# The first 100 microseconds of a one-core encoder layer: queue order of its loads, per-head constants, and the normed input in two VectorE operations

## Chip, cores, metric

The kernel runs on one core of a Trainium2 chip. The metric is the device time of one execution in microseconds, lower is better. A core has five instruction queues that matter here: TensorE (PE, matrix products), VectorE (DVE), ScalarE (ACT), GpSimd (POOL) and SyncE (SP, which in this kernel issues the DMA transfers). Each runs its own instructions in order and waits for the others through semaphores.

## What is computed

One layer of an encoder over 1024 tokens of 1024 channels. A conditioning vector c gives six modulation vectors, x is normed and modulated, and one wide projection feeds a sparse attention branch and a state-space (SSD) branch; then come a merge and a feed-forward part. What the change touches is the first lines:

```python
mod = (jax.nn.silu(c) @ ada_w + ada_b)[:, None, :]
shift_m, scale_m, gate_m, shift_f, scale_f, gate_f = jnp.split(mod, 6, axis=-1)
h = rmsnorm(x, pre_norm_mix) * (1.0 + scale_m) + shift_m
proj = h @ w_in
...
dt = jax.nn.softplus((dt_raw + dt_bias).astype(jnp.float32))
A = -jnp.exp(a_log.astype(jnp.float32))
...
y = (y_diag + y_off).reshape(Bsz, L, SSD_HEADS, SSD_HEADDIM) + d_skip[:, None] * xh
```

`dt_bias`, `a_log` and `d_skip` are the per-head constants, 32 numbers each.

## The kernel before

The kernel holds activations transposed: channels on the 128 partitions, tokens along the free axis. x and h are 8 tiles k = 0 to 7 of 128 channels, each in two halves b of 512 tokens. Products run in a split form: a float32 operand is kept as a high part (rounded to `F32R`, made by ScalarE) and a low part (operand minus high part), and three matmuls, high x high, high x low, low x high, give one product.

The beginning works tile by tile. For each k:

- `k_load(k)` issues three transfers on SP: two of 512 KB with the modulation weights that give scale and shift of tile k (`ada`), and one of 192 KB with tile k of the projection's first 384 columns (`p1raw`). The `ada` tiles come from an arena R of 8 slots, two per k, so the loads of k+4 wait until the matmuls of k have read theirs.
- `k_ada(k)` (through `ada_mm`) multiplies silu(c) with these weights on PE: 16 records in the profile; ScalarE copies the result (`adaacc`).
- `k_mod(k)` (through `ada_end`) sums it up by four tiny matmuls and writes `mod` (shift) and `amul` (gain times 1+scale) on DVE; it then splits `p1raw` into `p1h` (ACT) and `p1l` (POOL).
- `k_h(k, b)` makes the normed input: x times the spread 1/rms `rx[b]` (DVE), the high part `h..h` = x*amul+mod (ACT), the same sum in float32 (DVE), and the low part `h..l` (DVE for b = 0, POOL for b = 1).
- `k_mm(k, b)` accumulates nine matmuls into three PSUM banks (`pp`).

`rx[b]` needs the sums of squares of all eight tiles of that half (`x_squares`, `rstd`, `rspread`), with a power on POOL (`r`). Half 0 is ready first; k = 0 and 1 are done for it alone, then for half 1, and from k = 2 on both halves run in one loop.

Behind the beginning come the other columns of the projection. Their weights are streamed (class `Stream`, called `W`: load `wraw`, high part `whi` on ACT, low part `wlo` on POOL, with 4, 3 and 3 buffers; `uraw`, `uh`, `ul` are the like for a smaller array). `ada_slow` makes the later modulation vectors from `adaw` loads with products on POOL.

What sets the order: a scheduler orders each engine's instructions from dependencies and its own timeline simulation. In the block of the beginning, `in_order(*ORDERED)` chains PE, ACT and DVE to the order in which the code is written. `barrier` names one instruction per engine, and everything wrapped in `behind(...)` (the W stream, the small weights, the `adaw` loads) is put after it on that engine. The barrier stands on SP at the last `k_load`, on ACT and POOL at `k_h(5, 1)`. POOL and SP are not chained in the beginning: what is not named in a barrier may be moved.

`const_loads()` loads the causal mask and the per-head constants in five transfers, straight behind the second half of x. The two of `d_skip` read every second of 32 numbers for each of 64 partitions.

Of the kernel before, what the change touches and what calls it, by code (L numbers as in the profile page):

```python
# [10 lines left out]
F32 = mybir.dt.float32  # L11
# [57 lines left out]
def build(tc, a, dbg=None, stop=99, slots=None):  # L69
# [23 lines left out]
    def f(x):  # L93
        return x.bitcast(F32)
# [91 lines left out]
    ident = con.tile([P, P], F32, name="ident")  # L186
    mask384 = con.tile([P, 384], F32, name="mask384")
    tri = mask384[:, 0:128]
    dtb = con.tile([P, 32], F32, name="dtb")
    alb = con.tile([P, 32], F32, name="alb")  # L190
    dsk = con.tile([P, 16], F32, name="dsk")
    ones = con.tile([P, P], F32, name="ones")
    V.memset(ones, 1.0)
    nhalf = con.tile([P, 8], F32, name="nhalf")
# [117 lines left out]
    def ada_slow(j):  # L312

        acc = EV("adas", (P, 2, P))
        for h in range(2):
            t = wp.tile([P, 4, P], F32, name="adaw", tag="adaw", bufs=2)
            behind(SP.dma_start(t, a["ada_w"][j - 16][:, 4 * h:4 * h + 4]))
            G.tensor_tensor(t, t, cs[:, 4 * h:4 * h + 4, None].to_broadcast([P, 4, P]), op=OP.mult)  # L318
            V.tensor_reduce(acc[:, h], t.rearrange("p k m -> p m k"), axis=AX.X, op=OP.add)
        G.tensor_tensor(acc[:, 0], acc[:, 0], acc[:, 1], op=OP.add)  # L320
        return j, acc[:, 0]

    AHEAD = 2
    X0 = [[None, None] for _ in range(KT)]
    rx, Hs, first = [None, None], [([None, None], [None, None]) for _ in range(KT)], {}

# [12 lines left out]
            sums[k % 2] = sq  # L339

    def k_load(k):
        ts = [R(f"ada{k}", (P, 4, 256)) for _ in range(2)]
        for i in range(2):
            SP.dma_start(ts[i], a["ada_p"][k][i])
        raw = EV("p1raw", (P, 3, P))
        i = SP.dma_start(raw, a["w_p1"][k])
        first[k] = ts, raw
        return i

    def k_ada(k):  # L350
        first[k] = ada_mm(k, first[k][0]), first[k][1]
# [1 line left out]
    def k_mod(k):  # L353
        acc, raw = first[k]
        ada_end(k, acc)
        first[k] = split(Q, raw, "p1", (P, 3, P), lo_eng=G)

    def k_h(k, b):
        x = X0[k][b]
        V.tensor_tensor(x, x, rx[b], op=OP.mult)  # L360
        hi, lo = H_(f"h{k}h", dt=F32R), H_(f"h{k}l", dt=F32R)
        i1 = S.activation(hi, x, AF.Identity, bias=mod[:, k:k + 1], scale=amul[:, k:k + 1])
        V.tensor_scalar(x, x, amul[:, k:k + 1], mod[:, k:k + 1], op0=OP.mult, op1=OP.add)
        i2 = (G if b else V).tensor_tensor(lo, x, f(hi), op=OP.subtract)
        if k == 5:
            barrier.update((i.ins.engine, i.ins.name) for i in (i1, i2))
        Hs[k][0][b], Hs[k][1][b] = hi, lo
        dump("h", x, (k, slice(None), half(b)))

    def k_mm(k, b):  # L370
        for i, (wi, xi) in enumerate(((0, 0), (1, 0), (0, 1))):
# [1 line left out]
                T.matmul(pp1[t][b], first[k][wi][:, t, :], Hs[k][xi][b], start=k == 0 and i == 0, stop=k == KT - 1 and i == 2)  # L373

    def const_loads():
        SP.dma_start(mask384, a["mask384"])
        SP.dma_start(dtb, a["dt_bias"][None, :].to_broadcast([P, 32]))
        SP.dma_start(alb, a["a_log"][None, :].to_broadcast([P, 32]))
        for e in range(2):
            SP.dma_start(dsk[64 * e:64 * e + 64],  # L380
                         a["d_skip"].rearrange("(j e) -> e j", e=2)[e:e + 1, :].to_broadcast([64, 16]))

    x_load(0)
    SP.dma_start(ident, a["ident"])
    for k in range(AHEAD):
        k_load(k)
    x_load(1)
    const_loads()
    with in_order(*ORDERED):
        sums = [None, None], [None, None]  # L390
        x_squares(0, range(8), sums[0])
        r0 = rstd(sums[0], D)
        k_ada(0)
# [12 lines left out]
        k_mm(1, 0)
        r1 = rstd(sums[1], D)
        k_load(2)
        k_ada(2)
        pr1 = rspread(r1)  # L410
        rx[1] = Q("rx")
        S.activation(rx[1], pr1, AF.Copy)
        k_mod(2)
        k_h(0, 1)
        k_h(1, 1)
        k_mm(0, 1)
        k_mm(1, 1)
        for k in range(AHEAD, KT):
            k_h(k, 0)
            k_h(k, 1)  # L420
            if k < KT - 1:
                i = k_load(k + 1).ins
                barrier[i.engine] = i.name
                k_ada(k + 1)
            k_mm(k, 0)
            if k < KT - 1:
                k_mod(k + 1)
            k_mm(k, 1)
        nA = con.tile([P, 32], F32, name="nA")
        S.activation(nA, alb, AF.Exp)  # L430
# [1008 lines left out]
def arrays_of(inp):  # L1439
# [52 lines left out]
```

## Time and profile before

| | |
|---|---|
| median of 3 runs | 2513.75 us (2513.33 to 2513.93) |
| profiled execution, first to last instruction (span) | 2510.1 us; no other time of this execution is listed |
| PE busy | 2394.6 us, 95% of the span |
| DVE, ACT, POOL busy | 1512.3, 1213.8, 1003.9 us |
| the first of 40 slices of the span (63 us) | PE 4 tenths busy, all others 8 or 9 |

How to read the profile: the page gives the busy time of each engine, and the same over 40 slices of the span, a digit for tenths. The table of waits names who waited for whom, with the total in us, how often, and the longest. The timeline gives start and length in us, engine, source line, operation, output and inputs by the program's names, and in brackets the idle time of the engine before it with what ended it. A windows row gives, for one stretch, its length, the busy time of PE, weight loads, DVE, ACT and POOL (with instruction counts), the granted PE clock (1.00 is full), the share in which the 16 DMA engines were busy, and GB/s. A busy PE is not PE at its peak: at half clock it is as busy.

### The profile page before, as it was taken

To read this page: it belongs to the slowest core of one execution; us is meant where nothing else is said; L and a number is where in the kernel's file an instruction comes from. 1 tells how busy PE (TensorE), PEld (TensorE's weight loads), DVE (VectorE), ACT (ScalarE), POOL (GpSimd) and SP (SyncE) were. 2 spreads that over 40 slices of the span, in tenths; PEclk is the share of its full clock that TensorE was granted. 3 is DMA by queue.
4 is the path that set the end of the run, shared out by engine and by line. 5 is a ranking of instruction groups with operands and counts; after the bars stand their busy time and mean duration, and the time that the engine had idled before them with its cause. 6 is when DMAs were issued, how large, how long until landed. Compare 5 with 4: busy or idle time off the path is not lost. (4 is left out here: it accounts for less than half of the span.)

```text
span 2510.1 us, 34872 instructions
## 1 busy us (share of the span) xinstructions
PE 2394.6 (95%) x11946; PEld 1940.7 (77%) x11946; DVE 1512.3 (60%) x3056; ACT 1213.8 (48%) x2300; POOL 1003.9 (40%) x833
## 2 busy tenths in 40 slices
PE   4999999999989999999999999999999999999997
PEld 2788888888767787777776777878777888888886
DVE  3356777499766666866457677354376666442336
ACT  3355666467555665555656565444354222343111
POOL 1332112222443434522335435666576555432233
PEclk7999999999999999999999999999999999999998
DMA  6123212422322223312668885554464444243132
GB/s 243 40 84 130 74 63 76 151 93 97 118 97 91 91 95 123 106 39 69 190 219 283 278 263 179 190 190 135 137 215 157 162 147 143 89 163 131 47 101 89
DMA packets 213026, 338.11 MB, mean 135 GB/s; under 512 B 22976, under 2 KB 87152, under 8 KB 212848
## 3 DMA queue, kind: packets, MB, share of 16 engines
q1 hardware_dynamic: 212128, 335.30, 40.3%
q8 instruction: 94, 1.54, 0.2%
q14 instruction: 84, 0.69, 0.1%
q10 hardware_dynamic: 720, 0.58, 0.1%
HBM read 252.68 MB, written 86.27 MB: 135 GB/s over the span
## 5 line engine op out<-in xcount | busy, mean ns | idle before, releaser
L153 POOL TENSOR_TENSOR wlo<-wraw,whi 128x512 fp32r<-128x512 f32 (+1 forms) x282 | 379.4, 1347 | 761.8 <-ACT whi L152 702.5
L152 ACT ACTIVATE whi<-wraw 128x512 fp32r<-128x512 f32 (+1 forms) x282 | 175.4, 624 | 359.0 <-PE pfo L227 114.2
L1255 PE MATMUL p<-xh,wr 128*128 128x512 f32 x880 | 276.4, 392 | 5.7 <-DVE g L1305 4.2
L1249 POOL TENSOR_TENSOR wr<-a,wr 128x512 fp32r<-128x512 f32 x110 | 153.8, 1410 | 118.6 <-ACT wr L1248 76.6
L1255 PEld LDWEIGHTS p<-xh,wr 128*128 128x128 f32 x880 | 166.5, 189 | 41.7 <-DVE g L1305 4.6
L1255 PE MATMUL p<-xl,wr 128*128 128x512 f32 x440 | 172.2, 391 | 0.0
L779 ACT ACTIVATE lg<-lg,mx 128x256 f32<-128x256 f32 (+7 forms) x128 | 98.4, 770 | 92.3 <-DVE mx L776 90.0
L1248 ACT ACTIVATE wr<-a 128x512 fp32r<-128x512 f32 x110 | 67.9, 628 | 135.5 <-PE p L1255 110.4
L227 PE MATMUL pfo<-ah,wlo 128*128 128x512 f32 x304 | 118.1, 389 | 0.0
L227 PE MATMUL pfo<-al,whi 128*128 128x512 f32 x304 | 117.9, 389 | 0.0
L227 PE MATMUL pfo<-ah,whi 128*128 128x512 f32 x304 | 117.8, 389 | 0.0
L1255 PE MATMUL p<-h2h,wr 128*128 128x512 f32 x352 | 112.0, 394 | 0.0
L1370 DVE TENSOR_TENSOR facc<-facc,pfo 128x512 f32<-128x512 f32 x64 | 43.9, 687 | 112.0 <-PE pfo L227 112.0
L639 ACT ACTIVATE junk<-acc,cand__2203 128x1024 bf16<-128x1024 f32 (+2 forms) x96 | 86.2, 898 | 45.6 <-DVE cand__2203 L682 28.6
L800 PE MATMUL pt<-ident,lg 128*128 128x128 f32 x576 | 89.7, 279 | 15.2 <-ACT lg L779 14.0
L227 PE MATMUL pos<-yh,wlo 128*128 128x512 f32 x256 | 101.0, 395 | 2.7 <-POOL wlo L153 2.7
L227 PE MATMUL pos<-yh,whi 128*128 128x512 f32 x256 | 100.9, 395 | 1.7 <-ACT yh L1121 1.2
L590 DVE SCALAR_TENSOR_TENSOR acc<-rel,widx,acc 128x384 f32<-128x384 f32 (+2 forms) x90 | 87.0, 986 | 24.9 <-ACT rel L585 24.8
L585 ACT ACTIVATE rel<-prel 128x512 f32<-128x512 f32 (+3 forms) x160 | 77.2, 524 | 48.5 <-PE prel L584 45.0
L227 PE MATMUL pos<-yw,whi 128*128 128x512 f32 x256 | 100.3, 393 | 0.0
L318 POOL TENSOR_TENSOR adaw<-adaw,cs 128x512 f32<-128x512 f32 x64 | 68.6, 1075 | 70.2 <-DMA adaw<-ada_w 68.3
L1255 PEld LDWEIGHTS p<-xl,wr 128*128 128x128 f32 x440 | 83.2, 189 | 17.3
(568 smaller groups left out, 7023.7 us busy)
## 6 DMA issues: line engine op xcount, KB each, us to landing
wraw<-w_in SPq DMA_DIRECT2D x130, 256.0 KB, 2.7
a<-w_ffn_in SPq DMA_DIRECT2D x120, 256.0 KB, 3.0
adaw<-ada_w SPq DMA_DIRECT2D x64, 256.0 KB, 2.8
al<-d_ac SPq DMA_DIRECT2D x32, 512.0 KB, 5.7
wraw<-w_o_ssd SPq DMA_DIRECT2D x64, 256.0 KB, 3.0
al<-d_a SPq DMA_DIRECT2D x44, 256.0 KB, 4.9
d_a<-g SPq DMA_DIRECT2D x38, 256.0 KB, 2.0
ada<-ada_p SPq DMA_DIRECT2D x16, 512.0 KB, 7.4
```

Of the source, the lines that this page charges most:

```text
L152: behind(S.activation(hi[:, :kt], raw[:, :kt], AF.Copy))
L153: behind(G.tensor_tensor(lo[:, :kt], raw[:, :kt], f(hi[:, :kt]), op=OP.subtract))
L227: T.matmul(o, wt[:, k0 + i, :], xs[k][xi][b][:, sl], start=pi == 0 and i == 0 and wt is hi and xi == 0, stop=pi == len(pcs) - 1 and i == l ...
L318: G.tensor_tensor(t, t, cs[:, 4 * h:4 * h + 4, None].to_broadcast([P, 4, P]), op=OP.mult)
L585: S.activation(rel[:, 512 * b:512 * b + w_], pr[:, 0:w_], AF.Relu)
L590: V.scalar_tensor_tensor(acc[i][:, 0:n], rel[:, 0:n], ws, acc[i][:, 0:n], op0=OP.mult, op1=OP.add)
L639: S.activation(jk, y, AF.Sign, scale=-1.0, bias=a_, accum_out=o)
L779: S.activation(lg[:, 0:n], lg[:, 0:n], AF.Exp, scale=-1.0, bias=m, accum_out=mx[:, 3:4])
L800: T.transpose(ptv[:, hh, t, :], PR[hh, t][:, j * P:(j + 1) * P], ident)
L1248: S.activation(w[:, 0], src, AF.Copy)
L1249: G.tensor_tensor(w[:, 1], src, f(w[:, 0]), op=OP.subtract)
L1255: T.matmul(p, w[:, wi, i], X[x][i][xi], start=start and i == 0 and k == 0, stop=i == 3 and k == 2, skip_group_check=True)
```

## The change

- The three per-head constants become one array `heads` of 128 x 80 numbers, laid out on the host, so that one transfer of plain rows brings them; `dtb`, `alb`, `dsk` are slices of its tile. It and the mask are issued last, behind the weights of k = 7.
- SP is chained to the written order too, and four groups k are loaded ahead of the loop instead of two; in a group `p1raw` goes first.
- The normed input takes two DVE operations: x*amul*rx, and (x+mod)-high for the low part. ACT's high part adds `mod` alone. POOL makes no low parts of h any more.
- The barriers: on SP the last DMA of the last `k_load`; on ACT `k_h(6, 1)` instead of `k_h(5, 1)`; on POOL the last `p1l`, of k = 7. The POOL products of `ada_slow` now stand behind the barrier as well.

```diff
-            G.tensor_tensor(t, t, cs[:, 4 * h:4 * h + 4, None].to_broadcast([P, 4, P]), op=OP.mult)
+            behind(G.tensor_tensor(t, t, cs[:, 4 * h:4 * h + 4, None].to_broadcast([P, 4, P]), op=OP.mult))
...
-    AHEAD = 2
+    AHEAD = 4
...
     def k_load(k):
+        raw = EV("p1raw", (P, 3, P))
+        SP.dma_start(raw, a["w_p1"][k])
         ts = [R(f"ada{k}", (P, 4, 256)) for _ in range(2)]
         for i in range(2):
-            SP.dma_start(ts[i], a["ada_p"][k][i])
-        raw = EV("p1raw", (P, 3, P))
-        i = SP.dma_start(raw, a["w_p1"][k])
+            last = SP.dma_start(ts[i], a["ada_p"][k][i])
         first[k] = ts, raw
-        return i
+        return last
...
     def k_mod(k):
         acc, raw = first[k]
         ada_end(k, acc)
-        first[k] = split(Q, raw, "p1", (P, 3, P), lo_eng=G)
+        hi, lo = Q("p1h", (P, 3, P), F32R), Q("p1l", (P, 3, P), F32R)
+        S.activation(hi, raw, AF.Copy)
+        i = G.tensor_tensor(lo, raw, f(hi), op=OP.subtract)
+        barrier[i.ins.engine] = i.ins.name
+        first[k] = hi, lo
 
     def k_h(k, b):
         x = X0[k][b]
-        V.tensor_tensor(x, x, rx[b], op=OP.mult)
         hi, lo = H_(f"h{k}h", dt=F32R), H_(f"h{k}l", dt=F32R)
-        i1 = S.activation(hi, x, AF.Identity, bias=mod[:, k:k + 1], scale=amul[:, k:k + 1])
-        V.tensor_scalar(x, x, amul[:, k:k + 1], mod[:, k:k + 1], op0=OP.mult, op1=OP.add)
-        i2 = (G if b else V).tensor_tensor(lo, x, f(hi), op=OP.subtract)
-        if k == 5:
-            barrier.update((i.ins.engine, i.ins.name) for i in (i1, i2))
+        V.scalar_tensor_tensor(x, x, amul[:, k:k + 1], rx[b], op0=OP.mult, op1=OP.mult)
+        i = S.activation(hi, x, AF.Identity, bias=mod[:, k:k + 1])
+        V.scalar_tensor_tensor(lo, x, mod[:, k:k + 1], f(hi), op0=OP.add, op1=OP.subtract)
+        if k == 6:
+            barrier[i.ins.engine] = i.ins.name
...
     def const_loads():
+        SP.dma_start(heads, a["heads"])
         SP.dma_start(mask384, a["mask384"])
-        SP.dma_start(dtb, a["dt_bias"][None, :].to_broadcast([P, 32]))
-        SP.dma_start(alb, a["a_log"][None, :].to_broadcast([P, 32]))
-        for e in range(2):
-            SP.dma_start(dsk[64 * e:64 * e + 64],
-                         a["d_skip"].rearrange("(j e) -> e j", e=2)[e:e + 1, :].to_broadcast([64, 16]))
...
-    for k in range(AHEAD):
+    for k in range(2):
         k_load(k)
     x_load(1)
-    const_loads()
-    with in_order(*ORDERED):
+    for k in range(2, AHEAD):
+        k_load(k)
+    with in_order(*ORDERED, mybir.EngineType.SP):
...
-        k_load(2)
         k_ada(2)
...
-        for k in range(AHEAD, KT):
+        for k in range(2, KT):
             k_h(k, 0)
             k_h(k, 1)
+            if AHEAD <= k + 2 < KT:
+                i = k_load(k + 2).ins
+                barrier[i.engine] = i.name
+            if k + 2 == KT:
+                const_loads()
             if k < KT - 1:
-                i = k_load(k + 1).ins
-                barrier[i.engine] = i.name
                 k_ada(k + 1)
```

How this moves instructions shows at three places. First SP's queue behind the last transfer of x. Before, from there on (`dsk` are the two transfers of `d_skip`, the `ada` tiles 327 and 328 are of k = 2, 402 and 403 of k = 3, `wraw` and `uraw` are the later stage's weights):

```order
L376 DMA mask_90<-mask 128x384
L377 DMA dtb<-dt_bias 128x32
L378 DMA alb<-a_log 128x32
L380 DMA dsk<-d_skip 64x16x1 x2
L344 DMA ada_327<-ada_p 128x1024
L344 DMA ada_328<-ada_p 128x1024
L346 DMA p1raw<-w_p 128x384
L344 DMA ada_402<-ada_p 128x1024
L344 DMA ada_403<-ada_p 128x1024
L346 DMA p1raw<-w_p 128x384 x5
L151 DMA wraw<-w_in 128x512 x2
L167 DMA uraw<-w_qidx 128x512
```

Now, from the same place (`ada` 169 and 170 are of k = 2, 175 and 176 of k = 3, 397 and 398 of k = 4):

```order
L342 DMA p1raw<-w_p 128x384
L345 DMA ada_169<-ada_p 128x1024
L345 DMA ada_170<-ada_p 128x1024
L342 DMA p1raw<-w_p 128x384
L345 DMA ada_175<-ada_p 128x1024
L345 DMA ada_176<-ada_p 128x1024
L342 DMA p1raw<-w_p 128x384
L345 DMA ada_397<-ada_p 128x1024
L345 DMA ada_398<-ada_p 128x1024
```

and nine transfers further on, with the weights of k = 7 (`ada` 559 and 560):

```order
L345 DMA ada_559<-ada_p 128x1024
L345 DMA ada_560<-ada_p 128x1024
L377 DMA heads<-heads 128x80
L378 DMA mask_90<-mask 128x384
L151 DMA wraw<-w_in 128x512 x2
L167 DMA uraw<-w_qidx 128x512
L151 DMA wraw<-w_in 128x512 x2
L316 DMA adaw<-ada_w 128x512 x2
```

The constants went from ahead of k = 2 to behind k = 7, and the later stage's weights, which stood ahead of the `ada` tiles of k = 4 and more, now follow the constants.

Second, POOL from the `r` of half 1 on (`adaw` is `ada_slow`'s product, `h0l` to `h2l` are low parts of half 1). Before:

```order
L266 TENSOR_TENSOR r<-v,nhalf 128x4
L318 TENSOR_TENSOR adaw<-adaw,cs 128x512 x2
L248 TENSOR_TENSOR p1l<-p1raw,p1h 128x384
L364 TENSOR_TENSOR h0l<-x_153,h0h 128x512
L364 TENSOR_TENSOR h1l<-x_155,h1h 128x512
L364 TENSOR_TENSOR h2l<-x_157,h2h 128x512
```

Now:

```order
L265 TENSOR_TENSOR r<-v,nhalf 128x4
L357 TENSOR_TENSOR p1l<-p1raw,p1h 128x384 x6
L317 TENSOR_TENSOR adaw<-adaw,cs 128x512 x2
L153 TENSOR_TENSOR wlo<-wraw,whi 128x512 x2
L169 TENSOR_TENSOR ul<-uraw,uh 128x512
L153 TENSOR_TENSOR wlo<-wraw,whi 128x512 x4
```

The low parts of h are gone from POOL, and `adaw` and the W splits stand behind all `p1l`.

Third, ACT around tiles 5 to 7. Before:

```order
L302 ACTIVATE adaacc<-adap 128x256
L247 ACTIVATE p1h<-p1raw 128x384
L152 ACTIVATE whi<-wraw 128x512 x2
L168 ACTIVATE uh<-uraw 128x512
L152 ACTIVATE whi<-wraw 128x512
L362 ACTIVATE h6h<-x_136,mod,amul 128x512
L362 ACTIVATE h6h<-x_165,mod,amul 128x512
```

Now:

```order
L365 ACTIVATE h6h<-x_134,mod 128x512
L365 ACTIVATE h6h<-x_163,mod 128x512
L301 ACTIVATE adaacc<-adap 128x256
L356 ACTIVATE p1h<-p1raw 128x384
L152 ACTIVATE whi<-wraw 128x512 x2
L168 ACTIVATE uh<-uraw 128x512
L152 ACTIVATE whi<-wraw 128x512
L365 ACTIVATE h7h<-x_136,mod 128x512
```

The first splits of W moved from ahead of tile 6 to ahead of tile 7. On PE, four W matmuls now stand between the products of tile 6 and those of tile 7; behind the next stage's first tiles the order of every engine is the one before.

More of the change, by code (lines that the diff above doesn't have):

```diff
@@ L188, in build @@
     tri = mask384[:, 0:128]
-    dtb = con.tile([P, 32], F32, name="dtb")
-    alb = con.tile([P, 32], F32, name="alb")
-    dsk = con.tile([P, 16], F32, name="dsk")
+    heads = con.tile([P, 80], F32, name="heads")
+    dtb, alb, dsk = heads[:, 0:32], heads[:, 32:64], heads[:, 64:80]
     ones = con.tile([P, P], F32, name="ones")
@@ L355, in k_mod @@
         ada_end(k, acc)
-        first[k] = split(Q, raw, "p1", (P, 3, P), lo_eng=G)
+        hi, lo = Q("p1h", (P, 3, P), F32R), Q("p1l", (P, 3, P), F32R)
[3 more added lines that the diff above has]
+        first[k] = hi, lo
     def k_h(k, b):
         x = X0[k][b]
-        V.tensor_tensor(x, x, rx[b], op=OP.mult)
         hi, lo = H_(f"h{k}h", dt=F32R), H_(f"h{k}l", dt=F32R)
-        i1 = S.activation(hi, x, AF.Identity, bias=mod[:, k:k + 1], scale=amul[:, k:k + 1])
-        V.tensor_scalar(x, x, amul[:, k:k + 1], mod[:, k:k + 1], op0=OP.mult, op1=OP.add)
-        i2 = (G if b else V).tensor_tensor(lo, x, f(hi), op=OP.subtract)
-        if k == 5:
-            barrier.update((i.ins.engine, i.ins.name) for i in (i1, i2))
+        V.scalar_tensor_tensor(x, x, amul[:, k:k + 1], rx[b], op0=OP.mult, op1=OP.mult)
[3 more added lines that the diff above has]
+            barrier[i.ins.engine] = i.ins.name
         Hs[k][0][b], Hs[k][1][b] = hi, lo
-        dump("h", x, (k, slice(None), half(b)))
     def k_mm(k, b):
@@ L1466, in arrays_of @@
     out["vec"] = np.ascontiguousarray(np.concatenate([per_part(parts[n]) for n in COLS], 1))
-    for n in ("rel_bias", "dt_bias", "a_log", "d_skip"):
-        out[n] = np.ascontiguousarray(g[n])
+    out["rel_bias"] = np.ascontiguousarray(g["rel_bias"])
+    rows = np.concatenate([g["dt_bias"], g["a_log"]])[None, :]
+    skip = g["d_skip"].reshape(16, 2).T
+    out["heads"] = np.concatenate([np.repeat(rows, P, 0), np.repeat(skip, 64, 0)], 1)
     out["ident"] = np.eye(P, dtype=f32)
```

## Prediction

> **What bounds the kernel now.** First the page: how busy is TensorE (PE), and where not.
>
> ```profile
> span 2510.1 us, 34872 instructions
> PE 2394.6 (95%) x11946; PEld 1940.7 (77%) x11946; DVE 1512.3 (60%) x3056; ACT 1213.8 (48%) x2300; POOL 1003.9 (40%) x833
> ...
> PE   4999999999989999999999999999999999999997
> ```
>
> PE sets the end nearly everywhere, and the one slice far under nine tenths is the first, which the change edits. So I read PE's waits there (total, times, longest), and those from 105 to 600 us, to see whether a gain at the start is kept.
>
> ```profile
> PE adap L299 <- DMA ada<-ada_p: 12.9, 1, 12.9
> ...
> PE pp L373 <- POOL h0l L364: 9.4, 1, 9.4
> ...
> PE adap L308 <- ACT adaacc L302: 1.8, 1, 1.8
> PE pp L373 <- DVE h6l L364: 1.0, 1, 1.0
> ```
> ```profile
> PE pw L227 <- DVE cv L906: 0.9, 1, 0.9
> ```
>
> One wait for modulation weights, one for POOL, two small ones at tile 6; behind them 495 us with 0.9 us of waiting. From there on the order of every engine is what it was, so what is won earlier moves the rest forward whole.
>
> Why did the weights of k=2 come late? DMA-queue issues; landing times of `dsk`; packets of 22 to 38 us; two stretches whose last two numbers are DMA share and GB/s:
>
> ```profile
> 19.56 1.43 SPq L380 DMA_DIRECT2D dsk<-d_skip  x2
> 21.03 4.34 SPq L344 DMA_DIRECT2D ada<-ada_p  x2
> ```
> ```profile
> DMA to landing us min/median/max: 13.2/18.1/23.0
> ```
> ```profile
> DMA packets 1801, 0.03 MB, mean 2 GB/s; under 512 B 1795, under 2 KB 1800, under 8 KB 1801
> ```
> ```profile
> 4.00:22.00 18.00, 10.65 (x60) 7.64 (x61) 6.39 (x12) 8.66 (x16) 2.02 (x2) 1.00 1.00 359
> 22.00:38.00 16.00, 7.88 (x36) 6.54 (x34) 6.05 (x12) 4.35 (x9) 2.17 (x2) 0.74 0.05 2
> ```
>
> After 359 GB/s the transfers almost stop for 16 us: 1801 packets, nearly all under 512 B and 0.03 MB together, at a share of 0.05, about one engine of 16. They fit `dsk`, two issues of 64x16 single numbers, the last landing near 43 us; `ada` of k=2 was issued behind them at 21.03 and PE got it at 44.71. The timeline of PE, from three windows (start, length, line, operation, output<-inputs, count of matmuls; in brackets the idle time before and who ended it):
>
> ```profile
> 29.96 1.84 PE L261 MATMUL p<-ones,sq 128*128 128x1 f32 x16
> 44.71 2.30 PE L299 MATMUL adap<-ada,cs 128*32 128x256 f32 x16 [12.91 <-DMA ada<-ada_p]
> ...
> 50.60 1.65 PE L373 MATMUL pp<-h0h,p1h 128*128 128x512 f32 x3 [1.90 <-ACT h0h L362]
> ...
> 62.90 1.65 PE L373 MATMUL pp<-h0l,p1h 128*128 128x512 f32 x3 [9.37 <-POOL h0l L364]
> ...
> 67.89 1.07 PE L299 MATMUL adap<-ada,cs 128*32 128x256 f32 x16
> ```
> ```profile
> 91.57 1.07 PE L299 MATMUL adap<-ada,cs 128*32 128x256 f32 x16
> ```
> ```profile
> 114.08 0.39 PE L227 MATMUL pw<-h1h,whi 128*128 128x512 f32 x1
> ...
> 124.28 0.39 PE L227 MATMUL pw<-h4h,whi 128*128 128x512 f32 x1
> ```
>
> The holes are 31.8 (29.96+1.84) to 44.71 and 53.53 (62.90-9.37) to 62.90. `ada` marks the start of a round: 67.89 is k=3, 91.57 is k=7.
>
> **The change, part by part.**
>
> *Constants last, four groups in flight.* `dsk`, `dtb`, `alb` and `mask384` leave the middle of SP's queue and are put behind all eight weight groups; k=2 (2 x 512 KB + 192 KB = 1.25 MB) follows x directly. At 359 GB/s that is 3.5 us behind 22, so about 26, before PE needs it at 31.8. k=3 is there some 4 us later, k=4 to 6 wait only for tiles that `ada` of k=0 to 2 give back. The 12.9 us wait goes: **-12.9**; next late is `r` on POOL (below). `heads`, 320 B in each of 128 rows, and `mask384` now stand ahead of the first `w_in` loads; bounds nothing (other loads) to 23 us (`dsk`). I take nothing: W is first split behind tile 6, at about 67 us (below), and issued at about 43. `p1raw` ahead of `ada` adds 192 KB, 0.5 us at 359 GB/s, before k=0; no wait for `ada` stands there in the table of waits, so I take nothing of the 0 to 0.5.
>
> *Clock, first place.* Granted clock (the number before the DMA share):
>
> ```profile
> 29.00:30.00 1.00, 1.00 (x6) 0.77 (x4) 0.88 (x2) 0.00 (x0) 0.00 (x0) 0.61 0.05 0
> ...
> 32.00:34.00 2.00, 0.00 (x0) 0.00 (x0) 0.00 (x0) 0.00 (x0) 1.01 (x1) 0.80 0.05 0
> ...
> 67.00:68.00 1.00, 1.00 (x8) 0.54 (x10) 0.00 (x0) 0.00 (x0) 0.00 (x0) 0.84 0.00 0
> ```
> ```profile
> 98.00:99.00 1.00, 0.94 (x5) 0.94 (x5) 0.32 (x1) 0.42 (x2) 0.62 (x2) 0.52 0.34 121
> ...
> 104.00:105.00 1.00, 1.00 (x4) 0.77 (x4) 0.47 (x1) 1.00 (x1) 0.45 (x1) 0.57 0.00 0
> ```
>
> Each value is a mean of 0.5 and 1 over its stretch (0.80 over 32 to 34 is 1.2 us at 1, 0.8 at 0.5), which puts the steps at 29.8 (up), 33.2 (down), 67.3 (up), 98.0 (down), 104.9 (up): multiples of 3.41 us apart. Now the 16 `ada` matmuls of k=2 follow the sums at 31.8 while the clock is full: 1.07 instead of 2.30 us. POOL's `r` lands at 33.1 in either case:
>
> ```profile
> 32.08 1.01 POOL L266 TENSOR_TENSOR r<-v,nhalf 128x4 f32<-128x4 f32 x1 [7.38 <-DVE v L264]
> 58.64 2.04 POOL L318 TENSOR_TENSOR adaw<-adaw,cs 128x512 f32<-128x512 f32 x2 [25.55 <-DMA adaw<-ada_w]
> ...
> 61.58 1.26 POOL L364 TENSOR_TENSOR h0l<-x,h0h 128x512 fp32r<-128x512 f32 x1
> ...
> 91.95 2.70 POOL L153 TENSOR_TENSOR wlo<-wraw,whi 128x512 fp32r<-128x512 f32 x2
> ```
>
> so of the 5.9 us from `ada` to `h0h` (50.60-44.71) at best 1.4 go: 1.23 on `ada` less the wait for `r`, the rest on transposes and `ada_end`. The clock can fall in between, then nothing goes. Between 0 and 1.4 I take nearer the upper end, since the stretch behind 29.8 has no hole left: **-1.0**.
>
> *Low parts from POOL to VectorE, `adaw` behind the barrier.* POOL stood 25.55 us for `adaw`, with `h0l` queued behind; PE waited 9.4 for it. Now `h0l` is one VectorE operation right after `h0h`: **-9.4**. Per half and k VectorE runs two operations where it ran two (low part on POOL) or three:
>
> ```profile
> 50.58 0.55 DVE L363 TENSOR_SCALAR x<-x,amul,mod 128x512 f32<-128x512 f32 x1 [0.88 <-ACT h0h L362]
> ...
> 55.22 0.69 DVE L364 TENSOR_TENSOR h2l<-x,h2h 128x512 fp32r<-128x512 f32 x1
> ```
> ```profile
> 93.54 1.65 DVE L364 TENSOR_TENSOR h6l<-x,h6h 128x512 fp32r<-128x512 f32 x1
> 95.12 1.77 DVE L360 TENSOR_TENSOR x<-x,rx 128x512 f32<-128x512 f32 x1
> 96.92 0.81 ACT L362 ACTIVATE h6h<-x,mod,amul 128x512 fp32r<-128x512 f32 x1 [4.92 <-DVE x L360]
> ```
> ```profile
> L590 DVE SCALAR_TENSOR_TENSOR acc<-rel,widx,acc 128x512 f32<-128x512 f32 x15 | 11.2, 744 | 0.2 <-ACT rel L585 0.2
> ```
>
> The fused form isn't shown on x; its nearest row is the 128x512 one on `acc`, three operands in SBUF, 0.74; the bounds are 0.55 and 1.77 above. A half then costs 0.74+0.81+0.74 = 2.3 us in a row (ACT's step with a bias alone taken as 0.81 still). Counted from the first `h0h`, the high parts of k=1, 2, 2 stand at 2.3, 4.6 and 6.9 us; PE wants them at 3.7 or later, 6.8 and 9, so VectorE stays ahead. In the rounds of k=3 to 6 PE is gapless ((91.57-67.89)/4 = 5.9 us); VectorE's 2 x 2.3 + 0.4 is below: 0. If VectorE took over as the bound here, it would show as PE waits for the low parts.
>
> *Clock, second place.* The 18 matmuls of k=0 and 1 took 53.53-50.60 plus 67.89-62.90 = 7.9 us at half clock. The full-clock spacing is (124.28-114.08)/45 = 0.227 us. Without the holes one 3.41 us stretch (8 matmuls) should stay slow, then 10 x 0.227: 5.7. Bounds: all fast 4.1, all slow 7.9: **-2.2** (0 to -3.8). So `h0h` starts at 31.8+5.9-1.0 = 36.7, `ada` of k=3 at 42.4, of k=7 four rounds later at 66.
>
> *Barriers: W splits behind tile 7's `p1l` instead of tile 5.* At tile 6 POOL's splits slowed VectorE from 0.69 to 1.65 and 1.77, and PE then ran at half clock from 98.0 to 104.9. From 91.57 to 124.28, 32.7 us, PE has a round (5.9) and 90 matmuls (20.4), 26.3: 6.4 lost. The splits now meet tile 7. There `amul` (up to 0.8), x (1.77) and `h7h` (0.81) follow `ada_end` by 3.7 us; PE holds 9 + 4 matmuls, 2.95. With the low part, about 1.0 us of waits, too short to cool PE: **-5.4** (bounds 0 and -6.4). The Trainium skill (SBUF — State Buffer, "SBUF: two separate sides") speaks against this move: a VectorE operation with two SBUF inputs and a GpSimd operation exclude each other for whole instructions. By it an operation costs up to 0.69+1.35 = 2.04, an estimate that adds 0.3 us to each wait.
>
> Sum: 12.9+1.0+9.4+2.2+5.4 = 30.9. The execution shown spans 2510.1; no other time of it is listed, so I put around the span what the median has, 3.65. 2510.1-30.9+3.65 = 2482.85, which is 30.9 under the median of 2513.75.
>
> **The rivals.**
>
> 1. *The late weights were not `dsk`'s doing*, and PE still waits about 12.9 with a cold clock: 9.4+2.2+5.4 = 17.0, 2496.8. For it: packets carry no names. Against: only the four small constant loads stand there.
> 2. *Tile 7 pays what tile 6 paid*: VectorE loses the turn twice, PE cools, 5.4 is not won: 2488.2. For it: four operations meet ten POOL operations in a row. Against: PE holds 13 matmuls in between.
> 3. *The clock stays low up to k=3*: terms of 1.0 and 2.2 go, 2486.0. Its opposite, *no cooling at all* in gaps under 3.4 us: 1.4 and 3.8 instead, 2480.8. The row against it: down at 33.2 after 1.4 idle. That it cools only after an idle window is how the Trainium skill (TensorE: Matmul & The Clock Gate, Part 1) has it, with a free-running window of about 3.4 us; the grid agrees, the fall at 33.2 does not.
> 4. *Not faster: W starves.* In the fixed SP order its loads stand behind k=7, whose slot comes free only with `ada` of k=3, near 42 us, then `heads`, `mask384`. 3.3 MB at 359 GB/s are there by about 52. A delay costs from some 15 us on, and it takes 15+31 = 46 us, two `dsk`s in a row, to undo the gain: 2513 or more.
>
> **How the numbers follow.** Main case 0.64 (2479.5 to 2486.5: the bounds of the terms 1.0, 2.2 and 5.4 seldom all go one way), no cooling 0.08, low clock 0.10, tile 7 0.11, weights still late 0.05, starving 0.02. The range takes in all but the last two, and 3 us for how the later 2390 us answer: 2476 to 2490. A measurement of this kernel tells 0.2%, 5 us, from no change. Only starving ends there: faster 0.97, same 0.01, slower 0.02.
>
> **What the profile after would show.** Right: no wait for `ada` over 1 us at k=2, none for `h0l`; `ada` of k=3 near 42.5 (now 67.89), DMA busy without a hole to some 35 us; the matmul now at 124.28 near 93.5. Wrong: a hole in DMA behind x, waits at tile 7 over 2 us, or the later stages moved by another amount than the start.

## The result, and the profile after

| | before | after |
|---|---|---|
| median (range) | 2513.84 us (2513.33 to 2515.58) | 2481.34 us (2479.06 to 2483.61) |
| ratio, 95% interval | | 0.9864 (0.9852 to 0.9876) |
| span of the profiled execution | 2510.1 us | 2480.7 us |
| time of the profiled execution | not listed | 2482.46 us, 1.76 around the span |

The change made the kernel faster by 1.4%. The forecast was 2482.8. The kernel before lay between 2507.7 and 2518.3 us in the comparisons that follow, so single microseconds are read from the traces below, not from the times. (The medians differ by 32.5 us, the two profiled executions by 29.4.)

The page of after, and the table of PE's waits up to 115 us (total, times, longest):

```profile
PE 2391.6 (96%) x11946; PEld 1940.1 (78%) x11946; DVE 1508.6 (61%) x3048; ACT 1212.6 (49%) x2300; POOL 992.7 (40%) x825
...
PE   7999999999899999999999999999999999999996
```
```profile
PE p L260 <- DVE sq L337: 11.8, 1, 11.8
PE pp L374 <- ACT h0h L365: 2.1, 2, 1.9
PE pp L374 <- ACT h1h L365: 2.0, 1, 2.0
PE pp L374 <- ACT h7h L365: 0.4, 1, 0.4
```

The first slice went from 4 tenths to 7. The wait of 12.9 us for `ada` and that of 9.4 us for `h0l` are gone; what is left are the first sums, two waits of about 2 us that stood there before too, and 0.4 us at tile 7. The two stretches of DMA (last numbers: share of the 16 engines and GB/s):

```profile
4.00:22.00 18.00, 9.90 (x58) 7.09 (x59) 6.06 (x11) 7.95 (x15) 2.02 (x2) 1.00 1.00 365
22.00:38.00 16.00, 11.79 (x63) 9.52 (x62) 7.05 (x15) 6.97 (x14) 3.63 (x3) 0.78 0.99 378
```

From 22 to 38 us, where the transfers had run at a share of 0.05 and 2 GB/s, they now run at 0.99 and 378 GB/s. (The number before the share, the clock, has no records ahead of 24.2 us in after and is printed as 1.00 there; the 16 `ada` matmuls of k = 0 and 1 took 1.93 us each time, where full clock takes 1.07, so PE ran at half clock.) The timeline of PE, the rows that answer to those of before:

```profile
31.00 1.84 PE L260 MATMUL p<-ones,sq 128*128 128x1 f32 x16
32.77 1.07 PE L298 MATMUL adap<-ada,cs 128*32 128x256 f32 x16
34.18 0.95 PE L271 MATMUL prn<-ident,r 128*128 128x128 f32 x4 [0.34 <-POOL r L265]
...
37.65 1.65 PE L374 MATMUL pp<-h0h,p1h 128*128 128x512 f32 x3 [1.87 <-ACT h0h L365]
...
43.66 1.07 PE L298 MATMUL adap<-ada,cs 128*32 128x256 f32 x16
...
66.90 1.07 PE L298 MATMUL adap<-ada,cs 128*32 128x256 f32 x16
...
74.05 0.98 PE L374 MATMUL pp<-h7h,p1h 128*128 128x512 f32 x3 [0.39 <-ACT h7h L365]
...
93.71 0.39 PE L226 MATMUL pw<-h4h,whi 128*128 128x512 f32 x1
...
105.32 0.60 PE L271 MATMUL prn<-ident,r 128*128 128x128 f32 x4
105.67 0.48 PE L226 MATMUL pw<-h7h,wlo 128*128 128x512 f32 x1
```

The last row is the mark used from here on: a matmul behind the whole edited region, at 135.89 us before and 105.67 after. It came 30.2 us earlier; the prediction's sum was 30.9. The order is not quite the one before there: the four transposes of `prn` (0.35 us) stand ahead of the mark in after, and behind it in before. Counted alike it is 30.6 us, as the matmul that the prediction named has it: first `pw<-h4h,whi` at 124.28, now at 93.71 (forecast: near 93.5). Between the same pairs of rows in both traces:

| stretch on PE | before | after | change | predicted |
|---|---|---|---|---|
| start of `ada` k=2 | 44.71 | 32.77 | -11.9 | -12.9 |
| `ada` k=2 to `h0h` | 5.89 | 4.88 | -1.0 | -1.0 |
| hole before `h0l` | 9.37 | 0 | -9.4 | -9.4 |
| `h0h` to `ada` k=3, without that hole | 7.92 | 6.01 | -1.9 | -2.2 |
| `ada` k=3 to k=7 | 23.68 | 23.24 | -0.4 | 0 |
| `ada` k=7 to the mark | 44.32 | 38.77 | -5.6 (-5.9 counted alike) | -5.4 |

The spans differ by 29.4 us, so some 0.8 us (1.2 counted alike) was lost behind the mark, of 2375. Waits of PE that stand there in both traces are some longer, some shorter (for low parts of W on POOL 6.8 us in total instead of 5.1, for `lg` 11.5 instead of 14.0); which of them makes the loss was not settled.

At tile 7 VectorE meets POOL's splits, as forecast. VectorE's rows at tile 6 and tile 7, and the granted clock (before the DMA share) in four stretches:

```profile
67.41 0.75 DVE L364 SCALAR_TENSOR_TENSOR x<-x,amul,rx 128x512 f32<-128x512 f32 x1
...
70.82 0.89 DVE L309 SCALAR_TENSOR_TENSOR amul<-mod,vec 128x1 f32<-128x1 f32 x1
71.74 1.50 DVE L364 SCALAR_TENSOR_TENSOR x<-x,amul,rx 128x512 f32<-128x512 f32 x1
74.03 0.90 DVE L366 SCALAR_TENSOR_TENSOR h7l<-x,mod,h7h 128x512 fp32r<-128x512 f32 x1 [0.79 <-ACT h7h L365]
74.85 1.78 DVE L364 SCALAR_TENSOR_TENSOR x<-x,amul,rx 128x512 f32<-128x512 f32 x1
```
```profile
31.00:34.00 3.00, 2.84 (x33) 2.17 (x31) 0.16 (x1) 0.09 (x1) 0.88 (x1) 1.00 1.00 390
34.00:35.00 1.00, 0.82 (x6) 0.82 (x6) 0.00 (x0) 0.29 (x1) 0.13 (x1) 0.70 0.71 205
35.00:41.00 6.00, 4.13 (x13) 3.36 (x13) 3.57 (x7) 2.45 (x4) 1.44 (x1) 0.50 0.54 193
41.00:42.00 1.00, 1.00 (x6) 0.76 (x5) 0.25 (x1) 0.72 (x1) 0.00 (x0) 0.89 0.00 0
```

The fused operation takes 0.75 us alone (0.74 was taken) and 1.50 to 1.78 beside POOL's splits; PE, with the four W matmuls from 72.59 us on in hand, waited 0.4 us for that. The clock was full for `ada` of k=2, fell at 34.4 and came back at 41.2 us.

### The profile page after: what moved, and what is told of

Same layout as the page of the kernel before. It is cut to its first block, busy times and chain, and to the rows that moved or that the text cites. A ratio compares the mean times of both kernels' runs of the same rounds, so it can differ in the third digit from the quotient of the medians.

```text
span 2480.7 us, 34863 instructions
## 1 busy us (share of the span) xinstructions
PE 2391.6 (96%) x11946; PEld 1940.1 (78%) x11946; DVE 1508.6 (61%) x3048; ACT 1212.6 (49%) x2300; POOL 992.7 (40%) x825
## 5 line engine op out<-in xcount | busy, mean ns | idle before, releaser
L800 PE MATMUL pt<-ident,lg 128*128 128x128 f32 x576 | 90.2, 280 | 12.8 <-ACT lg L779 11.5
L905 DVE SCALAR_TENSOR_TENSOR cv<-pw,vec,cv 128x511 f32<-128x511 f32 (+2 forms) x96 | 71.2, 742 | 34.6 <-ACT cv L902 34.5
```

Source lines behind the costliest of these rows:

```text
L800: T.transpose(ptv[:, hh, t, :], PR[hh, t][:, j * P:(j + 1) * P], ident)
L905: V.scalar_tensor_tensor(ts[0][:, s:], p[0][:, :512 - s], w, ts[0][:, s:], op0=OP.mult, op1=OP.add)
```

## The experiments

In the expectations A is the attribution that the prediction made; the other letters are its rivals, each named below in words where a run bears on it. Each ratio is to the kernel before on the same chip.

| run | median, us | ratio (95%) | mark, us |
|---|---|---|---|
| e1_one_array | 2495.38 | 0.9929 (0.9914 to 0.9944) | 117.89 |
| e1b_array_behind | 2485.49 | 0.9891 (0.9874 to 0.9908) | 110.73 |
| e2_five_early | 2494.88 | 0.9932 (0.9914 to 0.9951) | 119.37 |
| e3_five_last | 2485.25 | 0.9887 (0.9872 to 0.9901) | 110.35 |
| e4_pool_low | 2485.52 | 0.9882 (0.9866 to 0.9899) | 106.89 |
| e5_adaw_free | 2483.33 | 0.9878 (0.9862 to 0.9894) | 103.69 |
| e6_barrier5 | 2483.74 | 0.9876 (0.9852 to 0.9900) | 105.63 |
| e9_three_ops | 2484.49 | 0.9884 (0.9869 to 0.9899) | 109.59 |
| e7_warm_start | 2478.40 | 0.9864 (0.9845 to 0.9884) | 103.47 |
| e8_warm_holes | 2473.77 | 0.9846 (0.9829 to 0.9863) | 101.06 |
| e10_ahead2 | 2479.92 | 0.9867 (0.9849 to 0.9884) | 104.19 |
| e0_after (after again) | 2480.21 | 0.9867 (0.9849 to 0.9885) | 105.41 |

The mark itself moves by about a microsecond between executions with the first sums: PE's first wait was between 11.1 and 12.0 us in these traces, except where that wait was filled. From `ada` of k=3 on it repeats: the four rounds take 23.24 us in after, e0, e2, e3, e6, e7, e8 and e10, and `ada` of k=7 to the mark 38.73 to 38.78 in after, e0, e2, e7, e8 and e10. The four transposes stand ahead of the mark in after, e0, e2, e3, e7, e8 and e10, and behind it in before, e1, e1b, e4, e5, e6 and e9; "counted alike" adds their 0.35 us to the latter.

**Before with the one array, in the old place (e1).** Only the five small loads become two; nothing is moved.

```diff
+        SP.dma_start(heads, a["heads"])
         SP.dma_start(mask384, a["mask384"])
-        SP.dma_start(dtb, a["dt_bias"][None, :].to_broadcast([P, 32]))
-        SP.dma_start(alb, a["a_log"][None, :].to_broadcast([P, 32]))
-        for e in range(2):
-            SP.dma_start(dsk[64 * e:64 * e + 64],
-                         a["d_skip"].rearrange("(j e) -> e j", e=2)[e:e + 1, :].to_broadcast([64, 16]))
```

> The kernel before, with one edit: the five small loads of the constants become one transfer of plain rows in the same place. Theory A (the element-wise load of d_skip stops the queue): the hole in DMA behind x goes, the weights of k=2 land near 26. But the scheduler now puts the two POOL products on adaw ahead of the r of half 1, and adaw's loads stand 23 transfers behind x, landing near 37; so r comes near 40 instead of 33, PE goes on about 6.5 us earlier than before, not 12.9, and the wait for h0l (9.4) goes too: about 16 us less, 2498 (2494 to 2501). Theory B (the weights are late because of the order of the queue and too few groups in flight, not because of d_skip): the hole stays and the time is that of before, 2513.8 within 2.

It was as expected: 2495.4, and the mark 18.0 us earlier. The wait for `ada` is gone though no load was moved, so the small loads were what held the weights of k=2. Of the five only `dsk` was late in before: `dtb`, `alb` and the mask landed 4.3 to 5.3 us after their issue, the two of `dsk` 13.2 and 23.0. Three rows of PE's waits, and two of POOL:

```profile
PE prn L271 <- POOL r L265: 6.3, 1, 6.3
...
PE adap L307 <- ACT adaacc L301: 1.8, 1, 1.8
PE pp L372 <- DVE h6l L363: 1.0, 1, 1.0
```
```profile
36.69 2.04 POOL L317 TENSOR_TENSOR adaw<-adaw,cs 128x512 f32<-128x512 f32 x2 [11.92 <-DMA adaw<-ada_w]
38.68 1.01 POOL L265 TENSOR_TENSOR r<-v,nhalf 128x4 f32<-128x4 f32 x1
```

The free `adaw` product, which no barrier holds, here stands ahead of `r` instead of `h0l`: POOL waits 11.92 us for its load, and PE 6.3 us for `r`. Tile 6 still waits, 1.8 and 1.0.

**The same, with the `adaw` product behind the barrier (e1b).** The low parts of the second half stay on POOL and the three operations stay.

```diff
-            G.tensor_tensor(t, t, cs[...], op=OP.mult)
+            behind(G.tensor_tensor(t, t, cs[...], op=OP.mult))
```

> The last one plus the products on adaw behind POOL's barrier: nothing else of the change (two groups ahead, three operations, low parts of half 1 on POOL, barriers at tile 5). Theory A: POOL's r comes at 33 and h0l follows h0h at once, so both large waits go without VectorE taking over the low parts: 12.9+9.4 and one or two us of clock, about 2490 (2487 to 2493); tile 6 still loses its 6. Theory B: 2513.8. Theory C (it takes VectorE's low parts to lose the wait for h0l): about 9 us more than A, 2499.

The median is 4.5 us better than A had it (2490), and outside its range. The mark came 25.2 us earlier, of the 30.6 of the whole change counted alike:

```profile
PE adap L307 <- ACT adaacc L301: 1.8, 1, 1.8
PE pp L372 <- DVE h6l L363: 0.5, 1, 0.5
```

There is no wait for `r` and none for `h0l`, with half of the low parts on POOL. The rival that the low parts' place on POOL made the 9.4 us falls here. Two of the edits together, one array and one `behind`, are worth about five sixths of the change. Part of it lies at tile 6, where neither edit was thought to act: `ada` of k=7 to the mark takes 42.25 us instead of 44.32, and the clock was at half there for 3.4 us (76.3 to 79.7) instead of 6.9.

**After, with the five small loads back behind x (e2).** `const_loads` is before's here, with a tile for each constant.

```diff
     x_load(1)
+    const_loads()
...
-            if k + 2 == KT:
-                const_loads()
```

> The changed kernel with one edit undone: the five small loads are back, in their old place behind x and ahead of the weights of k=2. Theory A: the hole of 16 us is back, PE waits some 12 us for the weights of k=2 and restarts at half clock: 2495 (2492 to 2498). Theory B: the fixed queue order and the four groups carry the gain, at most the 3 us of five more issues: 2481 to 2484.

It was as expected: the wait came back whole, and the mark 13.7 and 14.0 us later than in the two executions of after (the table's e0 is the second):

```profile
PE adap L299 <- DMA ada<-ada_p: 12.7, 1, 12.7
```
```profile
22.00:38.00 16.00, 8.95 (x38) 7.37 (x36) 5.83 (x12) 5.01 (x10) 2.19 (x2) 0.78 0.07 8
```

The DMA share of 0.07 over 16 us is back with them. With e1 this shows the small loads from both sides: taken out of before, put into after.

**After, with the five small loads last, where the array stands (e3).** The lines added are those that e1 takes away.

```diff
     def const_loads():
-        SP.dma_start(heads, a["heads"])
         SP.dma_start(mask384, a["mask384"])
+        SP.dma_start(dtb, a["dt_bias"][None, :].to_broadcast([P, 32]))
...
```

> The changed kernel with the five small loads instead of the array, but last, behind the weights of k=7, as the array is. It tells the place from the form. Theory A: the queue stops again for 16 to 23 us, now from about 45 on, and the first W loads, which stand behind, land near 62 to 68 instead of 53; ScalarE wants them at 69.5, so it costs at most 1 us: 2481 to 2483. If the form counts wherever it stands, 2490 or more.

This missed. The place alone doesn't cure it: the mark came 4.7 and 4.9 us later than after's two, and from `ada` of k=7 to the mark it is 44.29 us instead of 38.77. The two waits of PE that are new, ScalarE's row behind them, and the landing times of `dsk` and of all `wraw` loads:

```profile
PE pmi L227 <- POOL wlo L153: 2.6, 1, 2.6
...
PE pw L227 <- ACT whi L152: 1.3, 1, 1.3
```
```profile
71.30 1.30 ACT L152 ACTIVATE whi<-wraw 128x512 fp32r<-128x512 f32 x2 [2.54 <-DMA wraw<-w_in]
```
```profile
DMA to landing us min/median/max: 13.0/17.8/22.6
```
```profile
DMA to landing us min/median/max: 4.0/9.3/24.0
```

`dsk` blocks whatever is issued next on the queue, and here that is W: its first load took some 24 us to land, up to 71 us, and ScalarE wanted it at 68.8 (71.30-2.54). SP's issues behind it were held up too: the two `wraw` at 47.26 took 11.00 us to issue, and `uraw` came at 58.30. In after `heads` landed in 4.3 us:

```profile
DMA to landing us min/median/max: 4.3/4.3/4.3
```

The Trainium skill (DMA: Bandwidth & Descriptors, "Rules for kernel authors") says that a transfer whose last dimension is strided is cut into one descriptor per element. The trace of before agrees: two loads of 64 x 16 single numbers, and 1801 packets of which 1795 are under 512 B; the 16 us that these took are 8.9 ns for each.

**After, with the low parts of the second half on POOL (e4).**

```diff
-        V.scalar_tensor_tensor(lo, x, mod[:, k:k + 1], f(hi), op0=OP.add, op1=OP.subtract)
+        if b:
+            V.tensor_scalar(x, x, mod[:, k:k + 1], None, op0=OP.add)
+            G.tensor_tensor(lo, x, f(hi), op=OP.subtract)
+        else:
+            V.scalar_tensor_tensor(lo, x, mod[:, k:k + 1], f(hi), op0=OP.add, op1=OP.subtract)
```

> The changed kernel with the low parts of half 1 back on POOL (x+mod in one VectorE operation of its own, then the subtraction on POOL). Theory A (the wait for h0l was POOL standing for adaw, not POOL's 1.26 us for a low part): h0l lands near 39.6, PE wants it at 40.4; the rounds keep 5.8 us, h7l stands behind four splits and lands near 81 where PE wants it at 81.3: 2481 to 2484. Theory C (low parts belong on VectorE): waits of POOL come back in every round, 2488 or more.

POOL made `h0l` at 37.76 us with no wait of PE for it, there or later; the two waits at tile 7 grew from 0.4 to 0.9, and the mark is 1.2 and 1.5 us behind after's two, 1.6 and 1.8 counted alike:

```profile
PE pp L378 <- ACT h7h L365: 0.9, 2, 0.7
```
```profile
37.76 1.72 POOL L368 TENSOR_TENSOR h0l<-x,h0h 128x512 fp32r<-128x512 f32 x1 [0.50 <-DVE x L367]
```

The low parts' move to VectorE is worth about 1.9 us: 0.6 in the rounds, where `ada` of k=3 to k=7 takes 23.88 us instead of 23.24, and 1.3 from there to the mark (39.73, 40.08 counted alike, instead of 38.77), of which the waits at tile 7 are 0.5. `ada` of k=3 came 0.1 to 0.4 us earlier here. The median is 1.5 us above the expected range.

**After, with the `adaw` product free again (e5).**

```diff
-            behind(G.tensor_tensor(t, t, cs[...], op=OP.mult))
+            G.tensor_tensor(t, t, cs[...], op=OP.mult)
```

> The changed kernel without the barrier on the products on adaw. The scheduler then puts them ahead of the p1l of k=5, where their loads (near 52) are there in time, and tile 7 meets two POOL operations fewer. Theory A: no wait, 2480 to 2483. If the products stop POOL wherever they stand ahead of the rest, a wait of PE for p1l and 2484 or more.

On balance nothing was lost, though the median is 0.3 us above the expected range. The mark is 1.7 and 2.0 us earlier than after's two, 1.4 and 1.6 counted alike, and this is not the edit's doing: 0.7 to 0.9 is an earlier start, and 0.6 to 0.7 lies between `ada` of k=2 and of k=3, where the clock was at half for one stretch of 3.4 us instead of two. What the edit does evens out: the rounds take 23.91 us instead of 23.24, with a new wait of 0.4 us for `adaacc` beside the product, and `ada` of k=7 to the mark 38.04 counted alike instead of 38.77. POOL's product stands at 53 us and waited 1.62 us for its load, since the queue is no longer blocked:

```profile
53.34 2.49 POOL L317 TENSOR_TENSOR adaw<-adaw,cs 128x512 f32<-128x512 f32 x2 [1.62 <-DMA adaw<-ada_w]
```

In these runs the product did harm where its load was late. With the array in its new place the barrier on it is not needed; with the array in the old place (e1) it was worth 7.2 us of the mark (117.89 to 110.73).

**After, with the barriers of ScalarE and POOL one tile earlier (e6).** W's splits then meet tile 6, as in before. POOL's barrier, at `p1l`, is left out for k = 7.

```diff
-        if k == 6:
+        if k == 5:
             barrier[i.ins.engine] = i.ins.name
...
+        if k < 7:
             barrier[i.ins.engine] = i.ins.name
```

> The changed kernel with the barriers of ScalarE and POOL one tile earlier: the W splits stand ahead of tile 6, as in the kernel before, and the p1l of k=7 stands behind adaw and four splits. Theory A (the place of the splits cost the 6 us at tile 6, through VectorE and POOL taking turns): waits of 2 us and more at tiles 6 and 7, PE cools or not: 2484 to 2488. Theory D (two VectorE operations instead of three cured tile 6, the barrier did nothing): 2481.

The median, 2483.74, lies between the two theories, and the runs spread from 2477.8 to 2487.2, so the trace has to decide. The mark is at 105.63, counted alike 0.3 and 0.6 us behind after's two (105.67, 105.41). VectorE pays the same at tile 6 as after does at tile 7, yet PE waits little:

```profile
PE adap L307 <- ACT adaacc L301: 1.3, 1, 1.3
...
PE pp L375 <- ACT h6h L366: 0.3, 1, 0.3
```
```profile
65.02 1.50 DVE L365 SCALAR_TENSOR_TENSOR x<-x,amul,rx 128x512 f32<-128x512 f32 x1
...
68.12 1.78 DVE L365 SCALAR_TENSOR_TENSOR x<-x,amul,rx 128x512 f32<-128x512 f32 x1
```

From `ada` of k=7 to the mark it is 39.67 us, 40.02 counted alike (after 38.77, before 44.67 counted alike). A's loss is there to 1.3 us of 5.9: with two operations per half, and no low part of h on POOL, tile 6 is nearly cured without moving a barrier. Which of these two does it, e6 doesn't tell apart.

**After, with three operations, all on VectorE (e9).**

```diff
-        V.scalar_tensor_tensor(x, x, amul[:, k:k + 1], rx[b], op0=OP.mult, op1=OP.mult)
-        i = S.activation(hi, x, AF.Identity, bias=mod[:, k:k + 1])
-        V.scalar_tensor_tensor(lo, x, mod[:, k:k + 1], f(hi), op0=OP.add, op1=OP.subtract)
+        V.tensor_tensor(x, x, rx[b], op=OP.mult)
+        i = S.activation(hi, x, AF.Identity, bias=mod[:, k:k + 1], scale=amul[:, k:k + 1])
+        V.tensor_scalar(x, x, amul[:, k:k + 1], mod[:, k:k + 1], op0=OP.mult, op1=OP.add)
+        V.tensor_tensor(lo, x, f(hi), op=OP.subtract)
```

> The changed kernel with the normed input in three VectorE operations again (x*rx, then x*amul+mod, then the subtraction), all on VectorE for both halves. A half then takes about 2.75 us in a row, two halves and the small ones 5.9 against PE's round of 5.8. Theory A: VectorE just becomes the bound of the rounds, 0.1 to 0.5 us a round and up to 2 us at tile 7: 2482 to 2485. If ScalarE's and VectorE's chain stays hidden, 2481; if the fused form carried a large part, 2488 or more.

The time was as expected. `ada` of k=7 to the mark is 39.97 us, counted alike 1.6 more than after; the four rounds take 24.78 us instead of 23.24, since three operations per half make VectorE the bound there:

```profile
PE pp L375 <- DVE h7l L367: 1.3, 1, 1.3
PE adap L307 <- ACT adaacc L301: 1.0, 3, 0.3
```

With e6: each of the two, the later barrier (e9) and the two-operation form (e6), takes away most of the 5.9 us at the end of the region without the other; before had neither. In both the low parts of h are off POOL.

**After, with 34 products of ones on PE while it waits for x (e7), and with 7 more in each of two later holes (e8).** They write a bank that nobody reads. e7 has `fill(34)` alone, e8 all three lines.

```diff
+    def fill(n):
+        p = bank_d("fill")
+        for _ in range(n):
+            T.matmul(p[:, 0:P], ones, ones, start=True, stop=True, ...)
...
         sums = [None, None], [None, None]
+        fill(34)
...
+        fill(7)
         k_mm(1, 0)
...
         k_h(1, 1)
+        fill(7)
         k_mm(0, 1)
```

> The changed kernel with 34 more products of ones with ones at the very start, into a bank that nobody reads, so that PE is busy from about 1 us until the first sums at 11.8. Theory A (PE runs the first 30 us at half clock because it starts cold): the sums take 1.9 instead of 3.85, both ada groups 1.1 instead of 1.9, the nine products of k=0 2.1 instead of 3.9; x of half 1 lands by 23 and then bounds: 3 to 6 us less, 2476 (2474 to 2479). Theory E (PE waits for data there in any case): 2481 within 1.

> The last one with 7 more such products in each of the two later holes (ahead of the products of k=1 in half 0, and of k=0 in half 1). If a stretch with a hole of 2 us in it cools PE, as the fall of the clock at 33.2 in the kernel before says, filling them saves another 1.5 to 2.5 us: 2474 (2471 to 2477). If PE cools only after more than 3.4 us without work, nothing: the same as the last one, or a few tenths more.

e7's time was in its range, but the mark moved 1.9 us only (against e0 on the same chip), less than the 3 to 6 expected: the clock had fallen again when `ada` of k=1 came (its 16 matmuls took 1.93 us, the half-clock time). e8 hit: 2473.8, the mark 4.4 us before e0's, the fastest kernel of this study. Its runs lie between 2473.6 and 2478.8, those of after on the same chip between 2477.4 and 2483.6. Of the 6.4 us between the medians the region up to the mark accounts for 4.4; the rest isn't explained. PE's timeline in e8, and then the windows around the second hole, first of e7, then of e8:

```profile
32.53 1.81 PE L383 MATMUL fill<-ones 128*128 128x128 f32 x14
34.56 0.98 PE L374 MATMUL pp<-h0h,p1h 128*128 128x512 f32 x3 [0.22 <-ACT h0h L365]
...
39.04 1.07 PE L298 MATMUL adap<-ada,cs 128*32 128x256 f32 x16
```
```profile
33.00:40.00 7.00, 5.12 (x18) 4.17 (x17) 3.82 (x7) 3.11 (x5) 1.44 (x1) 0.59 0.61 238
```
```profile
29.00:40.00 11.00, 10.44 (x84) 7.77 (x84) 5.04 (x10) 3.56 (x6) 2.17 (x2) 1.00 0.77 300
```

The granted clock is 0.59 in e7 and 1.00 in e8. The 18 matmuls from `h0h` to `ada` of k=3 take 4.48 us in e8, 5.76 in e7 and 6.01 in after.

**After with two groups in flight instead of four, in the same order of the queue (e10), and after again (e0).**

```diff
-    AHEAD = 4
+    AHEAD = 2
...
+        k_load(2)
         k_ada(2)
...
-            if AHEAD <= k + 2 < KT:
-                i = k_load(k + 2).ins
+            if k + 1 < KT:
+                i = k_load(k + 1).ins
```

> The changed kernel with two groups ahead of the loop instead of four, each further group written one round earlier than it is used, and the queue still in the written order. The transfers then stand in the same order, and a queue entry waits only for its tile. Theory A: the number as such does nothing, 2481 within 2. If four groups in flight carry part of the gain, 2484 or more.

> The changed kernel once more, beside the variants of this chip: 2481.3 within 2.5, and the profile as before: no wait for the weights of k=2, tile 7 waiting 0.4 us.

2479.9 beside 2480.2: the number of groups in flight does nothing here. The marks differ by 1.2 us, of which 0.6 is the earlier start of `ada` of k=2 (32.00 and 32.59), and 0.6 lies between it and `ada` of k=3 (10.22 and 10.82), where the clock was at half for one stretch in e10 and for two in e0.

## Why the prediction was right, and where it was not

- **Constants last, -12.9.** Right in cause and nearly in size. The wait is gone whole; only 11.9 shows, since the sums ahead of it began at 31.00 instead of 29.96 us in this execution. e1 and e2, with the landing times, show `dsk` as the cause; rival 1 (another cause) is out. The heading is too narrow: the array cures this wait in the old place (e1), and the last place cures it for the five loads (e3), at a price further on. "Four groups in flight" had been put under the same heading and has no part in it (e10).
- **Clock, first place, -1.0.** Measured -1.0: `ada` at 1.07 us, then the fall of the clock in between, which the prediction had allowed for. Its reason for the upper end, that the stretch has no hole left, did not keep the clock up: it fell at 34.4 after 0.34 us of idle time. Rival 3 is out in both forms: the clock was full for `ada` of k=2, and it did fall after that.
- **"Low parts from POOL to VectorE, `adaw` behind the barrier", -9.4.** The size is right, the heading half wrong. The low parts' new place is worth about 1.9 us (e4), and not through this wait. What counts is that POOL doesn't stand waiting for `adaw` ahead of something that PE needs: the barrier ensures that (e1 against e1b), and so does a load that isn't late (e5).
- **The rounds, 0.** Measured -0.4. The step that VectorE's two operations stay ahead of PE held; no wait for a low part of the rounds stands in the table. e9 shows the other case, 1.5 us over four rounds.
- **Clock, second place, -2.2.** Measured -1.9. The step counted one slow stretch of 3.41 us inside the 18 matmuls. There were two in a row, from 34.4 to 41.2 us, and the second met the 18 matmuls almost whole.
- **Barriers, -5.4.** The size was near, 5.6 (5.9 counted alike), and the cause was half right. The prediction gave it to the splits' move from tile 6 to tile 7. The move is enough (e9), and it isn't needed: e6 undoes it and loses 1.3 us of 5.9 in that stretch. That VectorE's shorter chain is what bears POOL at tile 6 there is argued, not shown. At tile 7 the waits were put at 1.0 us and came to 0.4; rival 2 is out, and so are the 0.3 us more for each wait that the Trainium skill's whole-instruction lock (SBUF — State Buffer, "SBUF: two separate sides") had given as an estimate. VectorE's operations on x grew there by 0.75 and 1.03 us, less than the 1.35 of that estimate.
- **The offset, 3.65 us around the span.** Wrong: it is 1.76 in the execution shown and 1.76 to 1.82 in all four runs of after. So the execution of before that was profiled took about 2511.9 (2510.1+1.76), some 1.9 under its median. With 1.76 the sum gives 2481.0; with the measured 29.4 instead of 30.9 it gives the 2482.46 of the profiled execution. For this execution the two errors, 1.9 and 1.5, nearly cancelled, and the forecast's closeness is partly luck; the median, 2481.34, is 1.5 us under the forecast.
- **Rival 4 (W starves)** said that a delay of W costs from some 15 us on. e3's five loads cost 4.7 to 4.9 us of the mark: a load that is issued at 47 us and lands at 71 misses ScalarE's need at 68.8. In the change itself it didn't arise, since `heads` lands in 4.3 us. That number had been bounded by 0 and 23 and taken as harmless at either end; at 22.6 it isn't.

## What to carry to other kernels

Look in a starved stretch for one transfer made of single numbers: here it held back what stood behind it on its queue in both places where it was put, so change its layout first and its place second. Where one edit changes several things, the places in the trace tell what each place gains, not which part of the edit gains it; undoing the parts one by one does (two of six terms here had about the right size under a name that was wrong or half the story). An instruction that waits for a late load and isn't held by the order can land ahead of any other on its engine: fix the load, or pin the instruction.

## What was not expected of the hardware

The clock fell at 34.4 us in after, although PE had idled only 0.34 us in the 3.41 us before that, and no hole behind the first sums is over 2.0 us. What stood in those 3.41 us were matmuls of one column (16 in 1.84 us) and 16 with a weight tile of 32 columns, with the first of the transposes; in before, too, the fall at 33.2 followed the one-column sums and 1.4 us of idle time. The same instructions stand in e10, and there the clock did not fall in that place. Two stretches of 3.41 us of e10 and two of e1, each on the grid of the clock's own steps:

```profile
29.80:33.21 3.41, 3.27 (x35) 2.51 (x33) 0.16 (x1) 0.07 (x1) 0.86 (x1) 1.00 1.03 403
33.21:36.63 3.42, 1.32 (x9) 1.20 (x10) 1.36 (x4) 2.04 (x4) 1.30 (x2) 1.00 0.98 345
```
```profile
21.65:25.06 3.41, 1.85 (x11) 1.50 (x9) 2.82 (x6) 1.87 (x4) 1.17 (x1) 1.00 1.04 398
25.06:28.48 3.42, 2.20 (x9) 1.61 (x9) 2.50 (x5) 2.90 (x5) 0.00 (x0) 1.00 1.03 400
```

After the first of e10's, with 0.14 us idle and 1.67 of one-column matmuls, the clock stayed full; after the first of e1's it did so too, with 1.56 us idle and 0.34 of one-column matmuls. In after 0.34 and 1.68 made it fall, in e0 0.28 and 1.68, in e7 0.25 and 1.68. So neither decides alone; their sum does. In the first 75 us of the fourteen traces the clock fell after each of the 26 full-clock stretches with a sum of 1.93 us or more, and after none of the 130 with 1.90 or less. This is a count over these traces, with matmul ends that the profile models; it says nothing of other thin work, and it is not exact for the later stages (in after the clock also fell after a stretch from 679.5 us with 1.6 us idle). Where the grid lies against the first sums is a matter of the execution: e10 and e5 lost one half-clock stretch behind the second sums, after and e0 two.

That the clock halves only after an idle window of about 3.4 us (the Trainium skill, TensorE: Matmul & The Clock Gate, Part 1) doesn't fit: it fell after stretches with 0.25 to 0.35 us of idle time. The grid does fit, with steps at 27.6, 31.0, 34.4 and 41.2 in after, multiples of 3.4 us apart. Filling two holes of 2 us with dense products kept the clock full from 22.6 us on and brought the mark 2.4 us forward (e8 against e7).

A ScalarE operation with a bias alone takes 0.72 us where the one with scale and bias took 0.81; the prediction had left it at 0.81.
